# Cross-entropy over 32000 logits a row: loads that signal semaphores of the kernel itself, and picks sorted out ten groups at a time

## The chip, the cores and the metric

One NeuronCore of a Trainium2 chip. The metric is the device time of one execution in microseconds. The *span* is the part of it that the profile covers, from the first to the last recorded instruction; here it is about 2 us shorter than the time. ACT, POOL, DVE and SP are the profile's names of the core's ScalarE, GpSimd, VectorE and SyncE; SP issues the loads here, and 16 DMA engines move the data. A load is *issued* by SP and *lands* when all 16 have done their part of it; a semaphore, a counter that an engine can wait on, tells of the landing. (Each load has 16 landing records in the traces, and the 120 picks start 0.76 to 0.84 us after the last of the 16 in the kernel before.) An *instruction fetch* is a packet of the queue q14, whose kind the page gives as "instruction"; the seven within the span of the kernel before hold 8192 bytes each. That an engine gets the next piece of its program by it is inferred from the counts of executed instructions in the prediction.

## The reference

```python
# logits 16 x 512 x 32000 float32, labels 16 x 512
logits_max = np.max(logits, axis=-1, keepdims=True)
log_sum_exp = np.log(np.sum(np.exp(logits - logits_max), axis=-1)) + logits_max.squeeze(-1)
log_probs = logits - log_sum_exp[..., np.newaxis]
loss = -log_probs[np.arange(batch)[:, None], np.arange(seq), labels]
```

The 1048.6 MB of logits must be read once; everything else is small (the page before: 1048.64 MB read, 0.03 MB written).

## The kernel before

The 8192 rows lie as 64 groups of 128 partitions. A group is loaded in two halves of 16000 columns, each into one of three buffers of 64000 bytes a partition. ACT takes the exp in place and sums it in the same instruction (for 16000 columns 13.54 us; the profile shows a second, small one of 0.19 us that reads the accumulator). For 60 groups POOL picks the labels' logits out of the loaded half (an indirect copy of 48 candidates), and DVE sorts out, four groups at a time, which candidate is each partition's own. Four groups get their label logit by a gather from DRAM. The first and the last two groups are cut into smaller loads to shorten both ends.

```python
    data = ctx.enter_context(tc.tile_pool(name="data", bufs=3))
    NB = 4
    ...                                                          # cut
    for j, (g, b, at, n) in enumerate(loads):
        if b not in buffers:
            buffers[b] = data.tile([P, W], FP32, tag="t", name="t")
        t = buffers[b]
        c0 = col.get(g, 0)
        col[g] = c0 + n
        nc.sync.dma_start(out=t[:, at:at + n], in_=lg_pg[:, g, c0:c0 + n])
        if g in picked:
            ...                                                  # cut
            nc.gpsimd.indirect_copy(
                out=pk[:, 2 * i + h, :], data=t[:], idxs=lists[:, g, h, 0:3], i_know_this_is_slow=True
            )
        exp(g, t[:, at:at + n])
        if g in picked and h == 1 and i == NB - 1:
            nc.vector.copy_predicated(own[:], one_hot[:].unsqueeze(1).to_broadcast([P, NB * 2, NI]), pk[:])
            nc.vector.reduce_sum(out=found[...], in_=own[...], axis=X)   # shortened
```

The framework puts in the semaphores. A load increments one of eight landing semaphores ("lanes") in turn, and before a lane is used again SP waits for the landing of the load eight before (the trace has eight such semaphores, and 124 wait instructions at the line of the loads). A pick or exp that has more than one thing to wait for carries one wait and gets a wait instruction of its own, EVENT_SEMAPHORE in the trace, ahead of it for the rest (15 at the line of the picks, 128 at that of the exps).

The softmax here doesn't subtract the row's maximum and nothing guards it: scores larger than these inputs give would overflow.

Of the kernel before, what the change touches and what calls it, by code (L numbers as in the profile page):

```python
# [9 lines left out]
FP32 = mybir.dt.float32  # L10
# [3 lines left out]
EXP = mybir.ActivationFunctionType.Exp  # L14
# [6 lines left out]
def kernel(  # L21
# [6 lines left out]
    nc = tc.nc  # L28

    B, S, V = logits.shape  # L30
    P = 128
    G = B * S // P
    W = 16000
# [3 lines left out]
    lg_pg = lg.rearrange("(p g) v -> p g v", g=G)  # L37
# [17 lines left out]
    b = loads[-1][1] + 1  # L55
# [6 lines left out]
        loads.append((g, b + i, at, n))  # L62
    assert sum(l[3] for l in loads) == G * V

    data = ctx.enter_context(tc.tile_pool(name="data", bufs=3))
    persist = ctx.enter_context(tc.tile_pool(name="persist", bufs=1))


# [3 lines left out]
    NI = 48  # L72
    gathered = [0, G - 3, G - 2, G - 1]
    picked = [g for g in range(G) if g not in gathered]
    NB = 4
    assert len(picked) % NB == 0

    labs64 = persist.tile([P, G], mybir.dt.int64)
# [11 lines left out]
    lists = persist.tile([P, G, 2, 4], mybir.dt.uint16)  # L90
    own = persist.tile([P, NB * 2, NI], FP32)
    found = persist.tile([P, 2, G], FP32)
# [22 lines left out]
    for g in gathered:  # L115
        nc.gpsimd.indirect_dma_start(  # L116
            out=lab_logit[:, g:g + 1],
            out_offset=None,
            in_=lg,
# [6 lines left out]
    for q in range(3):  # L126
        nc.vector.tensor_scalar(  # L127
            out=mine[:, q:q + 1], in0=part16f[:], scalar1=4.0 * q, scalar2=None, op0=ALU.add
        )
    for n in (12.0, 6.0):  # L130
        nc.vector.tensor_scalar(  # L131
            out=mine_at[:], in0=mine[:], scalar1=n, scalar2=n, op0=ALU.is_ge, op1=ALU.mult
# [3 lines left out]
    for q in range(3):  # L136
        nc.vector.tensor_scalar(  # L137
            out=mine_at[:, q:q + 1], in0=mine[:, q:q + 1], scalar1=16.0 * q, scalar2=None, op0=ALU.mult
# [4 lines left out]
        out=one_hot[:], in0=entries[:], scalar1=at_entry[:], scalar2=None, op0=ALU.is_equal  # L143
    )
    nc.vector.tensor_scalar(
        out=clamped[:, 0, :], in0=labs32, scalar1=float(W - 1), scalar2=None, op0=ALU.min
    )
    nc.vector.tensor_scalar(
        out=clamped[:, 1, :], in0=labs32, scalar1=float(-W), scalar2=0.0, op0=ALU.add, op1=ALU.max
    )  # L150
    nc.vector.tensor_scalar(
        out=in_first[:], in0=labs32, scalar1=float(W), scalar2=None, op0=ALU.is_lt
    )
    for h in range(2):
        for q in range(3):
            nc.vector.tensor_scalar(  # L156
                out=lists[:, :, h, q], in0=clamped[:, h, :], scalar1=mine[:, q:q + 1], scalar2=None, op0=ALU.mult
            )
    nc.vector.memset(own[:], 0.0)  # L159


    buffers = {}
    col = {}
    n_exp = {}

    def exp(g, ap):
        k = n_exp.get(g, 0)
        n_exp[g] = k + 1
        s = sums[:, g, k:k + 1] if g < G - 1 else sums_last[:, k:k + 1]
        nc.scalar.activation(out=ap, in_=ap, func=EXP, accum_out=s)  # L170

    for j, (g, b, at, n) in enumerate(loads):
        if b not in buffers:
            buffers[b] = data.tile([P, W], FP32, tag="t", name="t")
        t = buffers[b]
        c0 = col.get(g, 0)
        col[g] = c0 + n
        nc.sync.dma_start(out=t[:, at:at + n], in_=lg_pg[:, g, c0:c0 + n])  # L178
        if g in picked:
            h = c0 // W  # L180
            i = picked.index(g) % NB
            if h == 0 and i == 0:
                pk = picks.tile([P, NB * 2, NI], FP32, tag="pk", name="pk")
            nc.gpsimd.indirect_copy(  # L184
                out=pk[:, 2 * i + h, :], data=t[:], idxs=lists[:, g, h, 0:3], i_know_this_is_slow=True
            )
        exp(g, t[:, at:at + n])
        if g in picked and h == 1 and i == NB - 1:
            nc.vector.copy_predicated(own[:], one_hot[:].unsqueeze(1).to_broadcast([P, NB * 2, NI]), pk[:])  # L189
            nc.vector.reduce_sum(  # L190
                out=found[:, :, g - NB + 1:g + 1].rearrange("p h g -> p g h"),
                in_=own[:].rearrange("p (g h) n -> p g h n", h=2),
                axis=X,
            )

        left = len(loads) - 1 - j
        if left == 9:
            nc.vector.reduce_sum(out=totals[:], in_=sums[:], axis=X)  # L198
            lo, hi = picked[0], picked[-1] + 1
            nc.vector.tensor_copy(out=lab_logit[:, lo:hi], in_=found[:, 1, lo:hi])  # L200
            nc.vector.copy_predicated(lab_logit[:, lo:hi], in_first[:, lo:hi], found[:, 0, lo:hi])  # L201
        if left == 8:
            nc.scalar.activation(out=logsum[:], in_=totals[:], func=LN)  # L203
            nc.vector.tensor_tensor(out=res[:], in0=logsum[:], in1=lab_logit[:, 0:G - 1], op=ALU.subtract)  # L204
        if left == 1:
            nc.vector.reduce_sum(out=part[:], in_=sums_last[:, 0:K - 1], axis=X)  # L206
# [36 lines left out]
```

## Time and profile before

| | before |
|---|---|
| median of the first 3 runs | 2431.07 us (2431.07 to 2431.30) |
| profiled run, its span | 2431.08 us, 2429.30 us |
| busy: ACT, POOL, DVE | 72%, 4%, 1% of the span |
| logits' queue on the 16 DMA engines | 99.8% of the span |
| recorded instructions | 954 |

The queues, the steady stretch and the waits are shown in the prediction. Three more views: first the chain of waits (start us, us, what), where it shows loads that landed later than the usual 41.57 us; the fourth late one is in the prediction:

```profile
321.45 41.57 DMA t<-in_logits_dram
378.21 41.69 DMA t<-in_logits_dram
...
831.99 41.80 DMA t<-in_logits_dram
...
1966.57 42.24 DMA t<-in_logits_dram
```

The groups of instructions: the two steps of the sort on DVE (count, busy us, mean ns, then the idle time before them).

```profile
L189 DVE COPY_PREDICATED own<-one_hot,pk 128x384 f32<-128x384 int32 x15 | 8.9, 593 | 2282.6 <-POOL pk L184 2282.6
...
L190 DVE TENSOR_REDUCE found<-own 128x8 f32<-128x384 f32 x15 | 8.3, 555 | 0.5
```

The timeline of the tail: the exp after which ACT has no more gap to the end (start us, us, engine, line).

```profile
2397.30 7.47 ACT L170 ACTIVATE t<-t 128x8720 f32<-128x8720 f32 x1 [2.54 <-DMA t<-in_logits_dram]
```

### The profile page before, as it was taken

Reading aid. Unit: us, or ns where it says so; the run is one execution under the profiler, and the core shown is the slowest. Engines: PE = TensorE matmul, PEld = TensorE weight load, DVE = VectorE, ACT = ScalarE, POOL = GpSimd, SP = SyncE. Lnnn points to the kernel's source line nnn. Section 1 sums busy time; section 2 is a strip of 40 time slices with the busy share of each in tenths; the row PEclk is TensorE's granted clock in tenths of the full one; section 3 lists DMA queues with packets and bytes.
Section 4 is the critical chain, followed back from the end, with each engine's and each line's share of the span. In section 5 each row is a group of like instructions: output and inputs, shape, how many; then the busy total and the mean of one; then the engine's idle time right before and its main releaser. Section 6 shows DMA issues by size and latency. Waiting matters only on the chain.

```text
span 2429.3 us, 954 instructions
## 1 busy us (share of the span) xinstructions
DVE 22.9 (1%) x63; ACT 1748.7 (72%) x281; POOL 86.7 (4%) x132
## 2 busy tenths in 40 slices
DVE  0000000000000000000000000000000000000000
ACT  4777767777677767777677776777667776777778
POOL 0000000000000000000000000000000000000000
DMA  9999999999999999999999999999999999999999
GB/s 423 436 424 438 438 426 434 438 433 427 438 437 424 437 437 432 429 438 434 426 438 436 431 431 437 433 428 437 436 428 435 434 435 428 437 436 426 437 429 382
DMA packets 20583, 1048.74 MB, mean 432 GB/s; under 512 B 2656, under 2 KB 2784, under 8 KB 3424
## 3 DMA queue, kind: packets, MB, share of 16 engines
q1 hardware_dynamic: 20304, 1048.62, 99.8%
q10 hardware_dynamic: 144, 0.07, 0.0%
q14 instruction: 7, 0.06, 0.0%
q0 software_dynamic: 128, 0.00, 0.0%
HBM read 1048.64 MB, written 0.03 MB: 432 GB/s over the span
## 4 chain that ended last, share of the span: by engine, by line
DMA 72%; ACT 24%; issue 2%; POOL 1%; POOLq 0%; SPq 0%; DVE 0%; ACTq 0%
DMA t<-in_logits_dram 72%; ACT t L170 24%; POOL pk L184 1%; POOLq L238 0%; SPq L178 0%; ACT logsum_last L210 0%; DVE res_last L211 0%; ACT logsum L203 0%; POOLq L184 0%; ACTq L170 0%
## 5 line engine op out<-in xcount | busy, mean ns | idle before, releaser
L170 ACT ACTIVATE t<-t 128x16000 f32<-128x16000 f32 (+6 forms) x139 | 1734.8, 12481 | 676.8 <-POOL pk L184 635.4
L184 POOL INDIRECT_COPY pk<-t,lists 128x48 f32 x120 | 81.7, 680 | 2216.4 <-DMA t<-in_logits_dram 2216.4
L189 DVE COPY_PREDICATED own<-one_hot,pk 128x384 f32<-128x384 int32 x15 | 8.9, 593 | 2282.6 <-POOL pk L184 2282.6
L170 ACT ACTIVATION_READ_ACCUMULATOR t<-t 128x1 f32 x139 | 25.9, 186 | 0.0
L190 DVE TENSOR_REDUCE found<-own 128x8 f32<-128x384 f32 x15 | 8.3, 555 | 0.5
L116 POOL DMA_INDIRECT lab_logit<-in_logits_dram,idx x4 | 4.1, 1032 | 1.3 <-issue 0.9
L109 ACT ACT_TABLE_LOAD x1 | 1.3, 1283 | 1.2 <-PEq L227 1.2
L198 DVE TENSOR_REDUCE totals<-sums 128x63 f32<-128x315 f32 x1 | 0.5, 481 | 80.9 <-ACT t L170 80.9
L156 DVE TENSOR_SCALAR lists<-clamped,mine 128x64 uint16<-128x64 f32 x6 | 1.2, 360 | 0.0
L112 POOL TENSOR_TENSOR idx<-idx,labs 128x64 int32<-128x64 int32 x1 | 0.3, 322 | 7.6 <-DMA labs<-in_labels_dram 7.6
L159 DVE MEMSET own<- 128x384 f32 x1 | 0.4, 378 | 0.0
L204 DVE TENSOR_TENSOR res<-logsum,lab_logit 128x63 f32<-128x63 f32 x1 | 0.2, 225 | 15.1 <-ACT logsum L203 15.1
L142 DVE TENSOR_SCALAR one_hot<-entries,at_entry 128x48 int32<-128x48 f32 x1 | 0.4, 354 | 0.1
L131 DVE TENSOR_SCALAR mine_at<-mine 128x3 f32<-128x3 f32 x2 | 0.3, 170 | 0.1
L110 DVE MEMSET sums<- 128x315 f32 x1 | 0.3, 321 | 0.9 <-PEq L227 0.9
L134 DVE TENSOR_TENSOR mine<-mine,mine_at 128x3 f32<-128x3 f32 x2 | 0.3, 161 | 0.1
L210 ACT ACTIVATE logsum_last<-sums_last,part 128x1 f32<-128x1 f32 x1 | 0.3, 294 | 0.0
L206 DVE TENSOR_REDUCE part<-sums_last 128x1 f32<-128x9 f32 x1 | 0.2, 162 | 14.5 <-ACT t L170 14.5
L137 DVE TENSOR_SCALAR mine_at<-mine 128x1 f32<-128x1 f32 x3 | 0.3, 146 | 0.0
L127 DVE TENSOR_SCALAR mine<-part16f 128x1 f32<-128x1 f32 x3 | 0.3, 147 | 0.0
L203 ACT ACTIVATE logsum<-totals 128x63 f32<-128x63 f32 x1 | 0.2, 238 | 0.0
L201 DVE COPY_PREDICATED lab_logit<-in_first,found 128x60 f32<-128x60 int32 x1 | 0.2, 231 | 0.0
(17 smaller groups left out, 2.6 us busy)
## 6 DMA issues: line engine op xcount, KB each, us to landing
t<-in_logits_dram SPq DMA_DIRECT2D x123, 8000.0 KB, 41.6
t<-in_logits_dram SPq DMA_DIRECT2D x1, 6000.0 KB, 36.8
t<-in_logits_dram SPq DMA_DIRECT2D x1, 5500.0 KB, 32.4
t<-in_logits_dram SPq DMA_DIRECT2D x1, 4500.0 KB, 24.2
t<-in_logits_dram SPq DMA_DIRECT2D x1, 4360.0 KB, 23.7
t<-in_logits_dram SPq DMA_DIRECT2D x2, 2000.0 KB, 9.7
t<-in_logits_dram SPq DMA_DIRECT2D x1, 4000.0 KB, 21.4
t<-in_logits_dram SPq DMA_DIRECT2D x1, 3235.0 KB, 31.0
```

The costliest lines, as they stand in the source:

```text
L109: nc.scalar.preload_act_table_set("natural_log_exp_and_others")
L110: nc.vector.memset(sums[:], 0.0)
L112: nc.gpsimd.tensor_tensor(out=idx[:], in0=idx[:], in1=labs32, op=ALU.add)
L116: nc.gpsimd.indirect_dma_start(out=lab_logit[:, g:g + 1], out_offset=None, in_=lg, in_offset=bass.IndirectOffsetOnAxis(ap=idx[:, g:g + 1], ...
L142: nc.vector.tensor_scalar(out=one_hot[:], in0=entries[:], scalar1=at_entry[:], scalar2=None, op0=ALU.is_equal)
L156: nc.vector.tensor_scalar(out=lists[:, :, h, q], in0=clamped[:, h, :], scalar1=mine[:, q:q + 1], scalar2=None, op0=ALU.mult)
L159: nc.vector.memset(own[:], 0.0)
L170: nc.scalar.activation(out=ap, in_=ap, func=EXP, accum_out=s)
L184: nc.gpsimd.indirect_copy(out=pk[:, 2 * i + h, :], data=t[:], idxs=lists[:, g, h, 0:3], i_know_this_is_slow=True)
L189: nc.vector.copy_predicated(own[:], one_hot[:].unsqueeze(1).to_broadcast([P, NB * 2, NI]), pk[:])
L190: nc.vector.reduce_sum(out=found[:, :, g - NB + 1:g + 1].rearrange("p h g -> p g h"), in_=own[:].rearrange("p (g h) n -> p g h n", h=2), a ...
L198: nc.vector.reduce_sum(out=totals[:], in_=sums[:], axis=X)
```

## The change

The intent: a pick (or, where there is none, an exp) should carry the landing of its load as its only wait, with no wait instruction ahead of it, and SP should not wait for lanes. The kernel allocates one semaphore for each of three fixed buffers, counts it up by 16 for each full-width load, and gives each short load a semaphore of its own. Sorting ten groups at a time makes it rarer that a pick must wait for DVE as well.

```diff
-    data = ctx.enter_context(tc.tile_pool(name="data", bufs=3))
+    data = ctx.enter_context(tc.tile_pool(name="data", bufs=1))
-    NB = 4
+    NB = 10
...
+    full_in = [tc.alloc_semaphore(f"full{i}_in") for i in range(3)]
+    n_full = [0, 0, 0]
+    spaces = [data.tile([P, W], FP32, tag=f"t{i}", name=f"t{i}") for i in range(3)]
...
-            buffers[b] = data.tile([P, W], FP32, tag="t", name="t")
+            buffers[b] = spaces[b % 3]
...
-        nc.sync.dma_start(out=t[:, at:at + n], in_=lg_pg[:, g, c0:c0 + n])
+        load = nc.sync.dma_start(out=t[:, at:at + n], in_=lg_pg[:, g, c0:c0 + n])
+        if n == W:
+            n_full[b % 3] += 1
+            loaded = (full_in[b % 3], 16 * n_full[b % 3])
+        else:
+            loaded = (tc.alloc_semaphore(f"short{j}_in"), 16)
+        load.then_inc(loaded[0], 16)
+        tc.no_tile_sem_insts.add(load.ins.name)
+        users = []
...
+            users.append(pick)
-        exp(g, t[:, at:at + n])
+        users.append(exp(g, t[:, at:at + n]))
+        users[0]._wait_ge(*loaded)
+        tc.add_to_no_dep_group(f"load{j}", load.ins)
+        tc.declare_no_dep(users[0].ins, load.ins, reason="waits for the load's own semaphore")
+        tc.declare_fence(users[0].ins, group=f"load{j}")
```

More of the change, by code (lines that the diff above doesn't have):

```diff
@@ L164 @@
     n_exp = {}
+    full_in = [tc.alloc_semaphore(f"full{i}_in") for i in range(3)]
+    n_full = [0, 0, 0]
+    spaces = [data.tile([P, W], FP32, tag=f"t{i}", name=f"t{i}") for i in range(3)]
+    exps = []
     def exp(g, ap):
@@ L169, in exp @@
         s = sums[:, g, k:k + 1] if g < G - 1 else sums_last[:, k:k + 1]
-        nc.scalar.activation(out=ap, in_=ap, func=EXP, accum_out=s)
+        return nc.scalar.activation(out=ap, in_=ap, func=EXP, accum_out=s)
     for j, (g, b, at, n) in enumerate(loads):
         if b not in buffers:
-            buffers[b] = data.tile([P, W], FP32, tag="t", name="t")
+            buffers[b] = spaces[b % 3]
         t = buffers[b]
@@ L183 @@
                 pk = picks.tile([P, NB * 2, NI], FP32, tag="pk", name="pk")
-            nc.gpsimd.indirect_copy(
+            pick = nc.gpsimd.indirect_copy(
                 out=pk[:, 2 * i + h, :], data=t[:], idxs=lists[:, g, h, 0:3], i_know_this_is_slow=True
             )
-        exp(g, t[:, at:at + n])
+            users.append(pick)
[4 more added lines that the diff above has]
+        tc.declare_fence(users[0].ins, group=f"load{j}")
+        exps.append(users[-1])
         if g in picked and h == 1 and i == NB - 1:
```

## The prediction

> **What bounds the kernel now.** I first read the page's slices, its queues and the share of the DMA engines. The lines are the busy tenths of the 16 DMA engines, what they moved in each fortieth of the span, and the queues (packets, MB, share of 16 engines).
>
> ```profile
> DMA  9999999999999999999999999999999999999999
> GB/s 423 436 424 438 438 426 434 438 433 427 438 437 424 437 437 432 429 438 434 426 438 436 431 431 437 433 428 437 436 428 435 434 435 428 437 436 426 437 429 382
> ...
> q1 hardware_dynamic: 20304, 1048.62, 99.8%
> q10 hardware_dynamic: 144, 0.07, 0.0%
> q14 instruction: 7, 0.06, 0.0%
> ```
>
> The logits' queue holds the DMA engines 99.8% of the span. ACT, the busiest compute engine, is at 72%. Second, the stretches view (us, busy time and instructions of DVE, ACT, POOL, then clock, DMA share, GB/s), which separates the steady part from the two ends:
>
> ```profile
> 80.40:2293.00 2212.60, 16.06 (x28) 1594.57 (x234) 79.59 (x117) 1.00 1.00 434
> ...
> 2420.00:2422.00 2.00, 0.00 (x0) 2.00 (x5) 0.00 (x0) 1.00 1.01 402
> 2422.00:2424.00 2.00, 0.00 (x0) 2.00 (x3) 0.00 (x0) 1.00 0.64 242
> ```
>
> The share is 1.00 for 2212.6 us, and the engines run out of data only at 2422 to 2424. Third, does any wait hold a load back? Here are the longest waits, the SP queue's own and POOL's, then the chain of waits around one load (start, us, what):
>
> ```profile
> SPq L178 <- ACT t L170: 2329.9, 126, 26.8
> SPq L178 <- DMA t<-in_logits_dram: 16.6, 2, 9.2
> ```
> ```profile
> POOL pk L184 <- DMA t<-in_logits_dram: 2216.4, 120, 47.0
> ACT t L170 <- POOL pk L184: 635.4, 120, 6.8
> ```
> ```profile
> 1115.70 41.57 DMA t<-in_logits_dram
> 1157.27 0.76 issue
> 1158.04 0.69 POOL pk L184
> 1158.73 0.02 issue
> 1158.75 13.64 ACT t L170 x2
> 1172.38 0.02 issue
> 1172.40 41.97 DMA t<-in_logits_dram
> ```
>
> A load lands, POOL starts its pick 0.76 us later, the exp and its accumulator read follow for 13.64 us, and only then does SP issue the next load of that buffer. That load lands 41.57 us after its issue, though in the timeline the picks start 18.9 us apart (99.22, 118.11, 137.01 us), so a load needs only 18.9 us of the engines. It therefore waits some 41.6 - 18.9 = 22.7 us behind earlier loads. Issuing it up to about 20 us sooner or later changes nothing. The 2329.9 us wait of SP is harmless, and so is every wait of POOL and ACT in this part. The kernel is bound by the DMA stream: its start, 1048.6 MB at 433.5 GB/s (8.192 MB in 18.90 us), and a tail.
>
> The tail: ACT is without a gap from the exp of the 8720 columns (2397.30) to the end. That exp starts when its data lands, so this last 29 us moves as one block with the stream.
>
> [...] the view of the source lines of the load, exp and pick lists (ns min/median/max, first and last start):
>
> ```profile
> L178 SPq EVENT_SEMAPHORE  x124: 17/17/17, 55.8 to 2374.9; - x124
> ```
> ```profile
> L170 ACTq EVENT_SEMAPHORE  x128: 17/38/38, 8.3 to 2414.6; - x128
> ```
> ```profile
> L184 POOLq EVENT_SEMAPHORE  x15: 17/17/17, 60.7 to 2178.9; - x15
> ```
>
> [...] So instruction fetches share the engines with the loads; the seven packets of q14 above show it. [...] In this trace each later fetch is one packet of 8192 bytes[...], and it is not hidden, because the DMA engines have no idle time.
>
> **The loss that the change can touch.** I went through the packet records and counted the instructions that each engine had recorded by each of the seven fetches. ACT had 63, 192 and 318 at 366.8, 1180.2 and 1974.6 us. SP had 80 and 208 at 723.3 and 1933.7. POOL had 66 at 820.7, DVE 61 at 1562.2. On ACT and SP a fetch comes about every 128 instructions (8192 / 128 = 64 bytes each). Chaining packets that follow one another shows the cost on the one DMA engine that serves a fetch: 0.30 us for the packet (0.309 us recorded), and the 64000-byte packet beside it takes 2.74 us instead of 2.366. That is 0.30 + 0.375 = 0.68 us per fetch. ACT's three fetches sit, as far as the chaining goes, on one DMA engine, so that engine falls 3 x 0.68 = 2.04 us behind. A load has landed only when all 16 engines are done, so the slowest sets all later landings. The chain shows it: loads landing after the fetches take 41.69, 41.80, 41.97 and 42.24 us instead of 41.57 (those after 366.8, 820.7, 1180.2 and 1974.6 us), together 1.42 us; it is less than 2.04 because other engines were behind from the start. The 41.97 quoted above is one of them.
>
> **The change part by part**, with counts from the two built programs:
>
> - SP: no more waits on the landing of the load eight before. EventSemaphores go from 136 to 7. 129 x 17 ns = 2.2 us of SP queue time, all under the 22.7 us of slack: 0 on the path. In the tail two such waits (16.6 us) go too; the last load, issued at 2404.9, can go at about 2388. It landed 20.4 us after issue, with data ahead of it all that time: 0.
> - ACT: 132 to 10. About 120 x 17 to 38 ns = 2 to 4.6 us of queue time, nearly all while the pick is awaited: 0. In the tail the exps keep the same waits, with the load's own semaphore in the place of the lane's: 0.
> - POOL: 22 to 13. A pick with two waits starts 0.06 us later (18.96 then 18.84 us apart, against 18.90). 9 fewer such: 0.5 us, under the slack: 0.
> - DVE: 15 sorts become 6, each 960 columns instead of 384. At 593 + 555 ns times 2.5 (an estimate by width) one is 2.9 us, six are 17.2 where 15 took 17.2. Two pick tiles alternate, so DVE has 20 loads (378 us) for each: 0. The wider memset ends near 14 us, well before the first pick at 61.5: 0.
> - Instructions to fetch: ACT's recorded 417 become 417 - 122 = 295, so the fetches at 63 and 192 stay and that at 318 goes. SP: 281 - 129 = 152, the one at 80 stays, that at 208 goes. POOL keeps its one. DVE: 88 - 27 = 61, its one goes or comes in the last microseconds. So 7 fetches become 4 or 5. On the slowest DMA engine one of three goes: -0.68 us. The SP and DVE fetches lie on engines that were ahead: 0.
>
> Sum: 2431.07 - 0.68 = 2430.4 us. The intent (cheaper waits) gives nothing by itself; the 0.03% comes as a by-product.
>
> **The rivals.**
>
> 1. The waits are on the path after all: each load gains 0.02 to 0.06 us of reaction, 125 x 0.02 to 0.06 = 2.5 to 7.5 us, so 2424 to 2429. For: the chain passes through every third pick and exp. Against: the same chain holds 41.57 us per load of 18.9, that is, a queue.
> 2. Nothing at all moves: another DMA engine is as late as ACT's (POOL's, say), or the fetch is tied to something other than the instruction count. Then 2431.1. For: the 820.7 us fetch was visible on the landings (0.23), so POOL's engine was behind too. Against: two later ACT fetches moved the landings by 0.40 and 0.67.
> 3. The stream gets worse: three semaphores shared by the buffers, or a fence that serialises loads. SP's order in the new program has each load waiting on ACT alone, as before, so the queue stays two deep[...]. I give that 1%.
> 4. The tail gets shorter by the early issue of the last loads: at most the last landing's wait of ACT, which I see as zero because ACT never idles there.
>
> **Range and chances.** Three runs before lie within 0.23 us. The expected effect is -0.68; with two fetches fewer on that engine it would be -1.36, with none 0. Some difference between chips is possible, so the range is 2429.6 to 2431.4 us. Faster by over 2% needs 48 us[...]: 0.003. Slower by over 2%: 0.01. Within 2%: 0.987.
>
> **What would show it.** Right: the logits' queue at 99.7 to 99.9%; the instruction queue at 4 or 5 packets; EventSemaphores almost gone on SP and ACT; loads still about 41.6 us from issue to landing and picks 18.9 us apart; DVE with 6 sorts of about 2.9 us or less; the exp of 8720 columns some 0.7 us earlier and the tail after it the same 29 us. Wrong: a landing time near 20 us (queue run dry), a DMA share under 1.00 in the steady stretch, seven fetches still, or a tail of another length. A gain of 2 us or more would mean that waits mattered.

The sum came to 2431.07 - 0.68 = 2430.4 us, worked out from the trace and the built programs. As for a difference between chips, the experiments ran on three, and the medians of the kernel before were 2431.06 to 2431.16 us.

## The result, and the profile after

The changed kernel took 2430.91 us (median of 6 runs, 2430.70 to 2431.25), the kernel before 2431.30 us in its runs (6, 2431.07 to 2431.43). The ratio is 0.9999, 95% interval 0.9986 to 1.0012: by the 2% rule the same. A ratio is the mean time of one kernel's fast runs over that of the other's of the same rounds, so not quite the ratio of the medians. Everything below is about fractions of a microsecond, under that interval; such readings rest on ranges that repeat within 0.1 to 0.5 us, and on what the traces record.

The page of the changed kernel, queues (packets, MB, share):

```profile
q1 hardware_dynamic: 20304, 1048.62, 99.9%
...
q14 instruction: 4, 0.03, 0.0%
```

Seven fetches within the span have become four. The DMA issues (count, KB each, us from issue to landing) and the SP queue's waits:

```profile
t<-in_logits_dram SPq DMA_DIRECT2D x123, 8000.0 KB, 41.6
```
```profile
SPq L184 <- ACT t L176: 2337.8, 126, 26.5
```

The landing time is still 41.6 us, and SP still waits as long in all: the slack stands as it was, and the two waits for landings (16.6 us) are gone from SP's list. The wait instructions ahead of the exps and of the picks (views of their source lines):

```profile
L176 ACTq EVENT_SEMAPHORE  x6: 17/17/17, 1.2 to 2410.0; - x6
```
```profile
L198 POOLq EVENT_SEMAPHORE  x6: 17/17/43, 12.5 to 1932.6; - x6
```

128 and 15 have become 6 and 6; SP's 124 at the loads are gone. The chain of waits, with a load of usual length for comparison:

```profile
340.12 42.05 DMA t<-in_logits_dram
...
1153.28 41.58 DMA t<-in_logits_dram
...
1380.07 42.00 DMA t<-in_logits_dram
...
1569.49 41.81 DMA t<-in_logits_dram
```

Three late loads where there were four, and 1.15 us of lateness in all instead of 1.42. The sort and the tail (groups of instructions, then timeline):

```profile
L209 DVE COPY_PREDICATED own<-one_hot,pk 128x960 f32<-128x960 int32 x6 | 7.4, 1233 | 2286.0 <-POOL pk L198 2286.0
...
L210 DVE TENSOR_REDUCE found<-own 128x20 f32<-128x960 f32 x6 | 6.9, 1155 | 0.2
```
```profile
2396.62 7.47 ACT L176 ACTIVATE t<-t 128x8720 f32<-128x8720 f32 x1 [2.53 <-DMA t<-in_logits_dram]
```

Six sorts of 2.39 us (the estimate by width was 2.9; nothing waits for them). The exp that opens the tail starts at 2396.62 instead of 2397.30, 0.68 us earlier. The span shrinks by 0.62 us (2429.30 to 2428.68). But the *time* of the profiled run shrinks by 0.21 only (2431.08 to 2430.87), and the medians by 0.39. Part of the gain went astray outside the span.

### The profile page after: what moved, and what is told of

Same layout as the page of the kernel before. It is cut to its first block, busy times and chain, and to the rows that moved or that the text cites. A ratio compares the mean times of both kernels' runs of the same rounds, so it can differ in the third digit from the quotient of the medians.

```text
span 2428.7 us, 667 instructions
## 1 busy us (share of the span) xinstructions
DVE 20.5 (1%) x45; ACT 1748.7 (72%) x281; POOL 86.7 (4%) x132
## 4 chain that ended last, share of the span: by engine, by line
DMA 71%; ACT 23%; issue 4%; POOL 1%; SPq 0%; POOLq 0%; DVE 0%
DMA t<-in_logits_dram 71%; ACT t L176 23%; POOL pk L198 1%; SPq L184 0%; POOLq L258 0%; ACT logsum_last L230 0%; DVE res_last L231 0%; POOLq L198 0%
## 5 line engine op out<-in xcount | busy, mean ns | idle before, releaser
L209 DVE COPY_PREDICATED own<-one_hot,pk 128x960 f32<-128x960 int32 x6 | 7.4, 1233 | 2286.0 <-POOL pk L198 2286.0
L210 DVE TENSOR_REDUCE found<-own 128x20 f32<-128x960 f32 x6 | 6.9, 1155 | 0.2
## 6 DMA issues: line engine op xcount, KB each, us to landing
t<-in_logits_dram SPq DMA_DIRECT2D x123, 8000.0 KB, 41.6
```

The lines of the kernel that those rows point to most:

```text
L210: nc.vector.reduce_sum(out=found[:, :, g - NB + 1:g + 1].rearrange("p h g -> p g h"), in_=own[:].rearrange("p (g h) n -> p g h n", h=2), a ...
```

## The experiments

The theory after the result: the time is that of the DMA stream; waits have 20 us of slack; what moves the end is how far the slowest of the 16 DMA engines has fallen behind through instruction fetches. The rivals: waits and their instructions do lie on the path, and fewer of them is the gain; what counts is the sum of fetched bytes; it is noise. Twelve runs in three calls; in each call the kernel before ran beside them (2431.13, 2431.16 and 2431.06 us, 9 runs each).

**The changed kernel once more**, unedited.

> The changed kernel once more, as the mark for the other runs of this call. Stream-and-fetch theory (the time is the DMA stream, held up only by instruction fetches on the slowest DMA engine; the waits are hidden): 2430.9 us, about 0.4 to 0.7 us under the kernel before, with four 8192-byte fetches within the span, two of them for ACT. Rival 'noise': no steady difference from the kernel before; the rounds overlap and the sign changes.

Measured: 2430.86 us (2430.67 to 2430.95), before 2431.13 (2431.01 to 2431.50). The ranges do not overlap: about 0.3 us, again. Four fetches within the span.

**The semaphore part alone.**

```diff
-    NB = 10
+    NB = 4
```

> The semaphore part alone: the loads' own semaphores, but the picks sorted out four groups at a time as before. Stream-and-fetch theory: ACT still has 295 recorded instructions and two fetches, SP one; DVE has its fetch back, on another DMA engine. So the same as the changed kernel, 2430.9 us within 0.3. Rival 'the rarer sort is what helps' (picks that also wait for DVE are on the path): back at the kernel before, 2431.3.

Measured: 2430.38 us (2430.29 to 2430.72), *faster* than the whole change. Neither expectation had that.

**The sorting part alone.** The kernel before with

```diff
-    NB = 4
+    NB = 10
```

> The sorting part alone: ten groups at a time, with the framework's landing semaphores as before. Stream-and-fetch theory: ACT keeps about 417 recorded instructions and three fetches, so the kernel before, 2431.3 us within 0.3. Rival 'the rarer sort helps': 2430.9.

Measured: 2431.62 us (2431.43 to 2431.76), slower than the kernel before by 0.49. So the whole gain is the semaphore part's, and the sorting part gives some of it back, in both surroundings by about 0.5 us. Why is settled below ("Outside the span").

**Eight wait instructions more per load on ACT.** Two waits are packed into one instruction, hence 16 (984 in all for 123 loads, by the built program):

```diff
+        if n == W:
+            for _ in range(16):
+                nc.scalar.wait_ge(*loaded)      # already satisfied
```

> The changed kernel with 8 wait instructions that are already satisfied after each full-width exp on ACT (984 in all). Stream-and-fetch theory: ACT goes from 295 to about 1279 recorded instructions, from two fetches to about ten, all on one DMA engine: 8 x 0.68 = +5.4 us, so 2436.3, while the waits' own time (8 x 17 to 38 ns a load) stays hidden. Rival 'waits are on the path': 123 x 8 x 17 to 38 ns = +17 to +37 us, 2448 to 2468. Rival 'fetches are hidden as well': 2430.9.

Measured: 2436.50 us (2436.35 to 2436.59), +5.6 on the changed kernel, where 8 x 0.68 = 5.4 was expected. Its page, and the late loads in its chain of waits:

```profile
q14 instruction: 12, 0.10, 0.0%
```
```profile
113.35 42.09 DMA t<-in_logits_dram
340.66 42.25 DMA t<-in_logits_dram
624.84 42.21 DMA t<-in_logits_dram
```

Ten of the twelve fetches come each time ACT has executed some 130 recorded instructions (60, 190, 320 and so on to 1220), and nearly every one makes a load land about 0.68 us late, 42.25 instead of 41.57. That is the size named in the prediction, ten times over. One reservation: the trace shows that these waits were executed beside the running exp, not after it (those in the chain after the exp of 384.39 us run from 384.47 to 384.97, and the exp's accumulator read starts at 397.83), so this run says nothing against the rival "waits on the path"; the run with the longer ACT work does.

**The same on SP**, eight per load:

```diff
+        if n == W and n_full[b % 3] > 1:
+            for _ in range(16):
+                nc.sync.wait_ge(loaded[0], loaded[1] - 16)   # already satisfied
```

> The changed kernel with 8 already satisfied wait instructions after each full-width load on SP (960 in all). Stream-and-fetch theory: SP goes from 152 to about 1112 recorded instructions, from one fetch to nine, on the DMA engine that serves SP: that engine is then 9 x 0.68 = 6.1 us late where ACT's was 1.4, so +4 to +5 us, about 2435.5. Rival 'waits are on the path': 120 x 8 x 17 ns = +16 us, 2447. Rival 'fetches are hidden': 2430.9.

Measured: 2435.45 us (2435.26 to 2435.51), as worked out from fetches. Of SP's nine fetches one comes only 1.1 us before the end of the span, after all the loads; each of the other eight made the picks 0.71 to 0.74 us later (the first 0.47).

**Half on ACT, half on SP** (8 of each of the two loops above).

> The same number of added wait instructions in all, but half on ACT and half on SP (4 a load on each). Stream-and-fetch theory with the slowest DMA engine deciding: ACT has six fetches instead of two, SP five instead of one, on two different DMA engines; only the later of the two counts: 4 x 0.68 = +2.7 us, 2433.6. Rival 'what counts is the sum of the fetched bytes': eight more fetches as in the run with all waits on ACT, +5.4 us, 2436.3. Rival 'waits on the path': +16 us or more.

Measured: 2433.68 us (2433.37 to 2433.84). This run has twelve fetches within the span, as many as each of the two runs before it, but the added ones fall on two DMA engines (six fetches of ACT's, five of SP's), and it costs +2.8 instead of +5.6 and +4.6 (against 2430.9 for the changed kernel). The rival of the sum of bytes is refuted; the slowest DMA engine decides.

**Longer work on ACT, three buffers.**

```diff
+        if n == W and g in picked:
+            nc.scalar.activation(out=t[:, 0:4000], in_=t[:, 0:4000], func=EXP, scale=0.0)
```

> The changed kernel with a further activation over 4000 columns (about 3.4 us) after each exp of a picked group, on data that is no longer needed, so each buffer comes free 3.4 us later. Stream-and-fetch theory: 22.7 us of slack becomes about 19: nothing but one more ACT fetch, +0.7 us at most, 2430.9 to 2431.6. Rival 'waits and the exp are on the path': 120 x 3.4 = +400 us or a good part of it.

Measured: 2431.54 us (2431.40 to 2431.56). Each buffer comes free some 3.5 us later 120 times, 420 us of additional work, and the cost is 0.6 to 0.7 us, that of one more ACT fetch (the trace has three, where the changed kernel has two). The landing time falls by 3.6 us (41.6 to 38.0), and the steady stretch is untouched (us, DVE, ACT and POOL busy, clock, DMA share, GB/s):

```profile
t<-in_logits_dram SPq DMA_DIRECT2D x123, 8000.0 KB, 38.0
```
```profile
80.40:2293.00 2212.60, 11.93 (x10) 2008.31 (x351) 79.39 (x117) 1.00 1.00 434
```

This is the run that refutes "waits and the exp are on the path": if 3.5 us a load cost nothing, neither do waits of 0.02 to 0.06.

It also answers a rival that the two main profiles leave open: in the changed kernel the first pick is 0.33 us earlier already, before any fetch, so the gain might come from the start. First and last start of the picks before, in the changed kernel and in this run:

```profile
L184 POOL INDIRECT_COPY pk<-t,lists x120: 673/680/702, 61.5 to 2312.0; 128x48 f32 x120
```
```profile
L198 POOL INDIRECT_COPY pk<-t,lists x120: 675/679/700, 61.2 to 2311.4; 128x48 f32 x120
```
```profile
L198 POOL INDIRECT_COPY pk<-t,lists x120: 674/679/701, 61.4 to 2312.0; 128x48 f32 x120
```

This run starts early and still ends as late as the kernel before: it too has three ACT fetches. The last pick starts at 2311.96 to 2312.06 us in the three profiles with three ACT fetches (the sorting part alone is the third) and at 2311.17 to 2311.50 in the six with two (added waits and the slower two-buffer runs left out). It goes with the fetches and not with the start.

**Two buffers in turn.** The third buffer serves only at the start and in the tail; `space(b)` gives the buffer in the place of `b % 3`:

```diff
+        if b < tail:
+            return (b + 1) % 2
...                                                              # cut: start and tail
```

> The changed kernel with two of the three data buffers in turn for the full-width loads (the third only at the start and in the tail). Stream-and-fetch theory: a load is issued 18.9 us later, so the time from issue to landing falls from 41.6 to about 22.7 us, and the DMA engines still have some 3.6 us of data ahead at each issue, against about 1 us from issue to first data: no gap, 2430.9 us within 0.5. Rival 'waits are on the path': with the slack cut by 18.9 us the wait for the pick and the exp shows, +0.3 us or more per load, over +35 us.

The "about 1 us from issue to first data" can be read at the start of the two main traces: the first load is issued at 0.74 us and its first packet starts at 1.74 before, 1.76 after.

Measured: 2478.51 us (2473.28 to 2484.51), +47.6: my expectation was a miss, and by number the rival's was met. The landing time is 23.5 us, as expected, and the DMA engines seem as busy as ever, but they move less:

```profile
t<-in_logits_dram SPq DMA_DIRECT2D x123, 8000.0 KB, 23.5
```
```profile
80.40:2293.00 2212.60, 11.94 (x10) 1564.14 (x229) 77.97 (x115) 1.00 1.00 425
```

The packet records show where. Between 600 and 1800 us, 1017 of 7960 packets of 64000 bytes took over 2.45 us (in the changed kernel 3 of 8128), and the mean rose from 2.365 to 2.412 us. Eight packets a load and engine make 0.37 us a load, times some 122 loads 45 us: the whole loss. Of the long packets 853 start within 2.2 us after the issue of a load, where only 128 packets are not long; they end about when the load ahead of it lands, so they are its last ones. The view's share counts a packet's whole duration as busy, so it cannot show this. New theory, inferred from these counts: a packet is slow when the DMA engine has nothing queued behind it yet as it starts, and here a load is issued only some 4.2 us (3.9 to 4.8) before the one ahead of it lands.

**Two buffers, exps cut short** (wrong results: 13000 of 16000 columns are summed; at the tolerance of the comparison it still passed):

```diff
-        users.append(exp(g, t[:, at:at + n]))
+        users.append(exp(g, t[:, at:at + (13000 if n == W and g in picked else n)]))
```

> Wrong results on purpose: the two-buffer kernel whose full-width exps of the picked groups cover 13000 of 16000 columns, about 2.5 us less, so each load is issued about 6.6 us before the one ahead of it lands, where it was about 4.1. Theory from the packets of the two-buffer run (the last packet of a load takes 2.5 to 3.0 us instead of 2.36 on each DMA engine when the next load was issued less than about 2 us before that packet starts): the long packets vanish, 2431 us within 1. Rival 'two buffers in turn are slow as such' (the addresses, one landing semaphore more often): stays at 2473 to 2485. Rival 'a chain of waits': two loads are shorter by 2.5 us at most until 18.9 a load is reached, also 2431, but then with long packets still there.

Measured: 2430.78 us (2430.75 to 2430.85), and 3 long packets of 8128. Two buffers are as good as three when the next load is issued 2.5 us earlier:

```profile
t<-in_logits_dram SPq DMA_DIRECT2D x123, 8000.0 KB, 25.2
```
```profile
80.40:2293.00 2212.60, 11.95 (x10) 1302.07 (x234) 79.82 (x118) 1.00 1.00 434
```

The addresses or the number of buffers are not the cause; how far ahead the next load is issued is. The limit lies between 4.2 us (23.5 - 19.3, the distance of the picks in the run before) and 6.3 us (25.2 - 18.9) ahead. That it is the empty queue which slows a packet is an inference; what these runs vary is the distance.

**Two buffers with the longer ACT work.**

> The two-buffer kernel with the further activation of about 3.4 us after each exp of a picked group; with three buffers that activation cost 0.4 to 0.7 us. A load is now issued only when the one before it is landing, so the DMA engines run dry: from the issue to first data about 1.0 us, then 18.9 us, then 0.4 us to the landing; two loads take 15.1 + 3.5 + 20.3 = 38.9 us, so 19.5 us a load. Expected: about 2431 + 120 x 0.57 = 2500 us (2480 to 2520), and, unlike in the two-buffer run, a DMA share clearly under 1.00 in the steady stretch. If every microsecond of exp counted in full, as 'waits and exp on the path' has it, it would be 2478 + 400.

The 1.0 us is the one above; for the 0.4 us, at the end of the two main traces the last packet of the last load of logits ends 0.44 us before that load's last landing record, in both.

Measured: 2566.76 us (2565.02 to 2569.35). The direction is right (share 0.97, dry engines), but I was 67 us too low: the landing time is 21.3 us, not the 20.3 of my sum. Two loads then take 15.1 + 3.5 + 21.3 = 39.9 us, and the picks in the trace are about 20.0 apart. Where the further microsecond goes was not followed up.

```profile
t<-in_logits_dram SPq DMA_DIRECT2D x123, 8000.0 KB, 21.3
```
```profile
80.40:2293.00 2212.60, 11.93 (x10) 1897.36 (x331) 75.83 (x111) 1.00 0.97 409
```

The same addition to ACT that costs 0.7 us with three buffers costs 88 us with two (2566.76 - 2478.51).

**The memset of the sorting tile moved to the start**, against the 0.5 us of the sorting part:

```diff
     nc.vector.memset(sums[:], 0.0)
+    nc.vector.memset(own[:], 0.0)
```

(and taken away where it was).

> The changed kernel with the memset of the wider sorting tile moved to the start, before the labels arrive and away from the four gathers. The sorting part alone was 0.5 us slower than the kernel before, and the semaphore part alone 0.5 us faster than the whole change. Theory 'the wider memset beside the gathers delays some DMA engine at the start': 2430.4. Rival 'chance of which DMA engine is behind after the start': 2430.9 within 0.3.

Measured: 2430.76 us (2430.69 to 2430.90), 0.1 under the whole change in another call; against the kernel before of its own call it is 0.30 lower, the whole change was 0.27. The memset beside the gathers is not the cause, or at most of 0.1 to 0.2 us.

**The semaphore part alone, again.**

> The semaphore part alone once more, in another call: does its 2430.4 us repeat (0.7 to 0.8 under the kernel before), or is it 2430.9 like the whole change? If it repeats, the sorting of ten groups costs about 0.5 us of what the semaphores gain, and this is the fastest version.

Measured: 2430.52 us (2430.46 to 2430.59), before 2431.06 (2430.96 to 2431.27). It repeats: this is the fastest version, by 0.5 to 0.75 us over the kernel before (0.02 to 0.03%) and by 0.3 to 0.5 over the whole change.

**Outside the span.** The profiled run of each kernel has a time and a span. Their difference, beside what the packet records hold after the last recorded instruction:

```
kernel                          time - span   8192-byte fetch after the end of the span
before (four groups)               1.78 us    none
semaphore part alone, two runs     1.78 1.77  none
changed, two runs (ten groups)     2.19 2.20  at +1.69, +1.68 us
sorting part alone                 2.20       at +1.68
eight other kernels, ten groups    2.19-2.20  at +1.67 to +1.95  (seven)
  the memset moved                 1.99       at +1.81
```

The other runs agree; the record gives their spans to 0.1 us: outside it lie 1.73 to 1.82 us in the 37 with four groups, 2.14 to 2.26 in the 48 with ten, and 1.96 to 2.15 in the five of the memset run. The median span of the sorting part alone is that of the kernel before, 2429.4 us; that of the semaphore part alone is that of the whole change, 2428.6. So the sorting part's 0.5 us lie outside the span, and the semaphore part's gain within it.

All eleven profiled runs with ten groups have one more instruction fetch just after the end, and 0.2 to 0.4 us more outside the span; the three with four groups have neither. DVE's instruction count fits: with four groups DVE has recorded 61 instructions when a fetch comes in the middle of the stream (1562 us; it moved a landing by at most 0.18 us, in one of three runs); with ten groups it has recorded 61 (in the memset run 60) in the whole span, and its next block is fetched only after the end (+1.67 to +1.95 us). That this fetch is DVE's is worked out from these counts, since a record does not name the engine. Within the span the counts can be checked: the packet of 64000 bytes beside a fetch takes 2.74 to 2.75 us where the count says ACT, 2.77 to 2.78 for SP, 2.71 to 2.72 for POOL and 3.02 for DVE, at every fetch beside the loads in the twelve profiles other than the two slower two-buffer ones. After the end no such packet runs. That a fetch there goes with 0.2 to 0.4 us, every profiled run shows. Whether the fetch causes them no run here separates.

## Why the prediction was right, and where a step was not

- **The number** tells little: 2430.9 us lies 0.5 above the 2430.4 of the sum, and the range of 2429.6 to 2431.4 also held the 2431.1 of "nothing moves". What speaks for the mechanism is what follows.
- **The bound and the hidden waits: right.** Share, landing time and SP's waits did not move; the run with 420 us more of ACT work in all cost 0.7 us.
- **"Issuing it up to about 20 us sooner or later changes nothing": too wide.** Issued 3.6 us later (38.0 us to the landing instead of 41.6) or 16.4 later (25.2), a load cost nothing but fetches; 18.1 later (23.5) cost 47.6 us. Some of the 22.7 us is needed as a lead.
- **No gain from SP's early tail loads: right.** SP's last load was issued at 2391.0 instead of 2404.9, and landed 33.7 instead of 20.4 us later. The tail kept its length: 32.00 us from the exp of 8720 columns to the end of the span before, 32.06 after.
- **The term -0.68 us: right within the span, though this one pair of profiles shows it only roughly.** The exp of 8720 columns is 0.68 us earlier and the span 0.62 us shorter; but the two differ by 0.33 us at the first pick already, and their late landings by 0.27 us only. Nine profiles give the size (see the run with three buffers and longer ACT work): with two ACT fetches the last pick is 0.66 us earlier on average than with three. ACT has two fetches instead of three, in all four fetches instead of seven. Landings at the last pick show it too: the slowest DMA engine was 1.9 us behind the median of the 16 before and is 1.4 us behind after, 0.5 us of the 0.68. The runs with added waits gave the same size per fetch (5.6 us for eight, 2.8 for four).
- **"DVE: ... its one goes or comes in the last microseconds", put at 0: wrong.** It came 1.7 us after the last recorded instruction, and there it goes with +0.4 us of time. With that the sum is -0.68 + 0.4 = -0.3, and 0.27 to 0.39 less were measured as medians. This term was missing, whatever its cause; it belongs to the sorting part alone, which I had put at 0 throughout.
- **"The SP and DVE fetches lie on engines that were ahead: 0": half wrong.** In the changed kernel the load after SP's fetch (1380.07) landed 0.43 us late, so SP's DMA engine was as far behind as ACT's at that moment. The second ACT fetch then added 0.24 instead of 0.68. The end is the same, because ACT's DMA engine leads again after its second fetch. Which engine is how far behind after the start differs from run to run: ACT's first fetch moved the landings by 0.48 in one run of the changed kernel and 0.24 in the other.
- **The instruction counts**: the remaining ACT fetches came at 46 and 174 recorded instructions, not at 63 and 192; the distance of 128 held, the start did not. Why the first came earlier by count stays open.
- **Rivals 1 and 4 fell, rival 2 was true for one fetch of SP's, rival 3 did not occur.** Of rival 3 the runs show what a shorter queue would have cost: +47.6 us at 4.2 us ahead. What it added of a queue one deep no run here showed; the shortest queue tried had loads landing 21.3 us after issue, 2.4 more than the 18.9 that they take of the engines.

## What to carry to other kernels

In a kernel whose DMA engines never pause (99.8% of the span here), ask of each change how it alters what the DMA engines carry, and of each wait how far ahead of need the next load is issued; 6.3 us ahead, the waits here cost nothing, and 4.2 us ahead was already too late. Instructions were DMA traffic too, 8192 bytes about every 128 recorded instructions of ACT: the fewer an engine executed, the fewer fetches delayed the one DMA engine that served it, by 0.68 us each, and the last load landed with the slowest. Look at time minus span as well, because what happens after the last recorded instruction is in the time (1.78 to 2.20 us here) and in none of the views used here.
